# Half of the down projection by seven products instead of eight, in parts of eight middle blocks

## The chip, the cores and the metric

The kernel runs on one core of a Trainium2 chip. Its engines go by the profile's names: PE is TensorE (matmuls; PEld loads their weights), DVE is VectorE, ACT is ScalarE, POOL is GpSimd and SP issues most of the transfers. The metric is device time in microseconds (us), the median of three runs.

## The reference, cut to what matters

Two layers work on 256 tokens of width 2048, all in float32. Each ends with a gated feed-forward block with 5632 middle columns:

```python
h2 = rms_norm(x, ln2_g[l])
u = depthwise_conv(h2 @ w_up[l], conv_w[l], conv_b[l])
gate, up = u[..., :D_FF], u[..., D_FF:]
x = x + (jax.nn.silu(gate) * up) @ w_down[l]
```

Ahead of it stand a norm, one input projection, two groups of attention heads and an output projection. The change touches only the last line, the down projection from 5632 middle columns to 2048 output columns.

## The kernel before

**Two parts of every number.** TensorE works on float32 in a reduced form (float32r). For full precision each operand is split into a high and a low part: `split` has ScalarE copy the source to the high part (L104, tile `whi` for weights) and VectorE subtract it from the source (L105, `wlo`). A product then takes three matmuls: high by high, low by high, high by low. `three` does so for the projections whose weights are the moving operand, with 512 columns each.

**Steps.** All large weights come as 1 MB loads (`quanta`, tile `raw`, three buffers). Each is used in two halves, the steps. `split_w` splits the weights of the step that is four ahead, with priority; `whi` and `wlo` have five buffers, so a split can begin when TensorE has left the step before the present one. The load three ahead is issued when both halves of a load are split.

**Feed-forward block.** The 5632 middle columns are 44 blocks of 128. A block f is made by `q_up` in four steps of 16 matmul pairs, then `glu` turns it into the middle block: ScalarE copies the product from PSUM (L505), VectorE adds and scales (L506, L507), POOL fills the borders of the convolution (L509, L510), ScalarE and VectorE do the convolution (L515, L517), the gate (L519) and the product (L520), and a split makes the two parts, tile `mid`. The down projection works on the four output blocks nb of 512 columns; per nb and pair of middle blocks a step has 12 matmuls (two token halves, two blocks, three products). It runs in chunks of `CHUNKS = (12, 12, 12, 8)` blocks, each chunk behind the up projections of its blocks and of one block more, so that the last block's `glu` is covered. After each nb VectorE adds the PSUM tile to x (`add_x`, L453). PSUM tile `mm` has two buffers of two banks and serves both projections. In the last chunk of a layer nb 0 and nb 1 take turns over the groups of four blocks, as no block follows:

```python
order = [(nb, g) for nb in range(NB) for g in range(ng)]
if end == NF:
    order = sorted(order, key=lambda o: (o[0] // 2, o[1], o[0]) if o[0] < 2 else (1, 0, 0))
```

At the end of the first layer `whole_x` adds to x, squares it and transposes it on TensorE for the next layer (`turn_x`, L140, tile `S`, then `prep_x`, L107 and L108). The order on each engine is set by a scheduler at build time, from the order of the code and the priorities; each engine then works strictly in that order.

Of the kernel before, what the change touches and what calls it, by code (L numbers as in the profile page):

```python
# [11 lines left out]
F32 = mybir.dt.float32  # L12
# [6 lines left out]
P = 128  # L19
# [11 lines left out]
FF = 5632  # L31
NF = FF // P
FG = 4
CHUNKS = (12, 12, 12, 8)
NB = 4
EPS = 1e-6
NEG = -1e30
# [14 lines left out]
def encoder_kernel(  # L52
# [91 lines left out]
    def stat_x(which):  # L144
        v = work.tile([P, TT], F32, name="ssum", bufs=2)
        nc.vector.reduce_sum(v, st["ss"], axis=AX.X)
        st["r1"] = act.tile([P, TT], F32, name="r1")
        rsqrt(v, 1.0 / D, st["r1"], "c2")
        if which == 1:

            d = work.tile([P, 4, HD], F32, name="tq", bufs=2)
            for tt in range(TT):
                nc.vector.tensor_scalar(d[:, tt], ident, st["r1"][:, tt:tt + 1], None, op0=ALU.mult)
            ps = psum.tile([P, T], F32, name="pv", bufs=1)
            mm(ps, ones, d[:, 0:TT].rearrange("p t d -> p (t d)"), True, True)
            st["r2"] = act.tile([P, T], F32, name="r2")
            nc.scalar.activation(st["r2"], ps, AF.Copy)

    def stat_o(grp):
# [197 lines left out]
    def values(l, grp, h):  # L357
        t = sm.pop(("T", grp, h))
        ps = psum.tile([P, T], F32, name="pv", bufs=1)
        if grp == "a":  # L360
            v, c = V["a", h // 4], (h % 4) * HD
            mm(ps[:, 0:KW], v[:, 0, c:c + HD], t[:, 0, 0:KW], True, False)
            mm(ps[:, T - KW:T], v[:, 1, c:c + HD], t[:, 1, 0:KW], False, True)
        else:
            v, c = V["b", 0], (h // 4) * HD
            for kt in range(TT):
                mm(ps, v[:, kt, c:c + HD], t[:, kt, :], kt == 0, kt == TT - 1)
        g = 0 if grp == "a" else 1
        if h == 0:
            acc_o[grp] = act.tile([P, T], F32, name=f"acc_{grp}")  # L370
        k = g * NH + h
        os[k] = act.tile([P, 2, T], F32R, name="mid", bufs=16)
        split(os[k][:, 0], os[k][:, 1], ps, par["on_g"][:, l, g, h:h + 1])
        add_square(acc_o[grp], ps, h == 0)

# [125 lines left out]
    def glu(l, f, ps):  # L501
        ux = halo[f % 2]
        r = T // GRID_W
        t = work.tile([P, 2, T], F32, name="prob", bufs=2)
        nc.scalar.activation(t, ps[:, :, 0], AF.Copy)  # L505
        nc.vector.tensor_add(t, t, ps[:, :, 1])  # L506
        nc.vector.tensor_mul(ux[:, :, r:r + T], t, st["r2"][:, None, :].to_broadcast([P, 2, T]))  # L507

        nc.gpsimd.tensor_copy(ux[:, :, 1:r], ux[:, :, T:T + r - 1])  # L509
        nc.gpsimd.tensor_copy(ux[:, :, T + r:T + 2 * r - 1], ux[:, :, r + 1:2 * r])  # L510
        y = work.tile([P, 2, T], F32, name="pT", bufs=4)
        for j in range(2):
            c = j * NF + f
            w0, w1, w2, b = (par["conv"][:, l, i, c:c + 1] for i in range(4))
            nc.scalar.activation(y[:, j, :], ux[:, j, r:r + T], AF.Identity, scale=w1, bias=b)  # L515
            for w, o in ((w0, 0), (w2, 2 * r)):
                nc.vector.scalar_tensor_tensor(y[:, j, :], ux[:, j, o:o + T], w, y[:, j, :],  # L517
                                               op0=ALU.mult, op1=ALU.add)
        nc.scalar.activation(t[:, 0, :], y[:, 0, :], AF.Silu)  # L519
        nc.vector.tensor_mul(t[:, 1, :], t[:, 0, :], y[:, 1, :])  # L520
        gs[f] = act.tile([P, 2, T], F32R, name="mid", bufs=16)
        split(gs[f][:, 0], gs[f][:, 1], t[:, 1, :])

    def q_down(l, c, nb, g):
        f0, nf = sum(CHUNKS[:c]), CHUNKS[c]

        def body(q, half, hi, lo):
            ps = banks(("dn", nb), g == 0 and half == 0)
            hv, lv = (w.rearrange("p (k n) -> p k n", k=2) for w in (hi, lo))
            i = FG * g + 2 * half  # L530
            three(ps, (gs[f0 + i], gs[f0 + i + 1]), hv, lv, i == 0, i == nf - 2,
# [19 lines left out]
    for l in range(L):  # L551
        for j in range(NJ):
            for u in range(4):
                quanta.append((a["w_in"][l, j, u], q_win(l, j, u), False))
        for grp in "ba":
            for nb in range(NB):
                for u in range(2):
                    quanta.append((a["w_out"][l, 0 if grp == "a" else 1, nb, u], q_wout(l, grp, nb, u), False))
        f = 0
        for c, nf in enumerate(CHUNKS):  # L560

            end = min(sum(CHUNKS[:c + 1]) + 1, NF)
            while f < end:
                for u in range(2):
                    quanta.append((a["w_up"][l, f, u], q_up(l, f, u), True))
                f += 1
            ng = nf // FG
            order = [(nb, g) for nb in range(NB) for g in range(ng)]
            if end == NF:
                order = sorted(order, key=lambda o: (o[0] // 2, o[1], o[0]) if o[0] < 2 else (1, 0, 0))  # L570
            for nb, g in order:
                quanta.append((a["w_down"][l, sum(CHUNKS[:c]) // FG + g, nb], q_down(l, c, nb, g), False))


    steps = [(q, h) for q in range(len(quanta)) for h in range(2)]

    raw, hl, left, loads, highs = {}, {}, {}, {}, {}

    def load(q, parts=1):
        if q < len(quanta):  # L580
            raw[q] = wp.tile([P, 2048], F32, name="raw", bufs=3)
            left[q] = 2
# [20 lines left out]

    xT = []
    for i in range(KD // 2):
        xT.append(act.tile([P, 2, T], F32, name="mid", bufs=16))
# [91 lines left out]
def _layout(inputs):  # L698
# [71 lines left out]
```

## Time and profile before

| | |
|---|---|
| median of three runs | 2126.24 us (2125.97 to 2126.32) |
| profiled execution, time | 2126.1 us |
| its span, first to last instruction | 2124.3 us |
| PE busy | 2118.1 us (100%) |
| DVE busy | 1458.0 us (69%) |
| ACT busy | 1141.2 us (54%) |
| feed-forward stretch of the first layer (345 to 1041 us): PE, DVE, ACT busy | 696.0, 477.6, 363.5 of 696.0 us |
| TensorE clock granted | 1.0 throughout |
| DMA | mean 187 GB/s |

Rows of a timeline give the start, the duration, the engine, the line, what is written from what, and in brackets the idle time before and what ended it. Groups give the busy time, the mean duration in ns and the idle time before. Matmul records overlap: a rate is read from starts. In an unmerged row x8 means eight instructions in a row.

### The profile page before, as it was taken

The page shows a single profiled execution, that of the slowest core. Times are in us where ns is not written, and L with a number is a line of the kernel's source. Part 1 is how long each engine was busy: PE and PEld are TensorE (multiplying, and loading weights), DVE is VectorE, ACT ScalarE, POOL GpSimd, SP SyncE. Part 2 cuts the span into 40 slices and gives each one's busy share as a digit, 9 for nine tenths or more (in the row PEclk, how much of TensorE's full clock was granted, in tenths as well). Part 3 has the DMA queues.
Part 4 walks back from the last instruction along what each step waited for, and adds up shares of the span by engine and source line. Part 5 has one row for each costly group of instructions (what it writes and reads, how often), then busy time and mean ns, then how long its engine had stood idle before and what let it go on. Part 6 is the DMA issues. An engine that isn't in the chain of part 4 may idle for free.

```text
span 2124.3 us, 28802 instructions
## 1 busy us (share of the span) xinstructions
PE 2118.1 (100%) x10904; PEld 1815.3 (85%) x10904; DVE 1458.0 (69%) x2293; ACT 1141.2 (54%) x1651; POOL 142.1 (7%) x215
## 2 busy tenths in 40 slices
PE   9999999999999999999999999999999999999999
PEld 8888888888888888888888888888888888888887
DVE  7777667775677577657756866677756775776575
ACT  7566556554455355535655665565544553555453
POOL 0000000110011011001000000001100100110010
PEclk9999999999999999999999999999999999999999
DMA  9544555555555555555555454555555555555554
GB/s 345 195 141 170 176 178 178 181 197 198 181 196 191 189 195 182 196 198 182 196 180 197 139 171 160 174 182 185 197 194 184 195 188 192 193 185 197 192 185 139
DMA packets 60843, 397.89 MB, mean 187 GB/s; under 512 B 7328, under 2 KB 9888, under 8 KB 13728
## 3 DMA queue, kind: packets, MB, share of 16 engines
q1 hardware_dynamic: 59696, 394.71, 54.3%
q8 instruction: 85, 1.39, 0.3%
q10 hardware_dynamic: 1008, 1.34, 0.2%
q14 instruction: 54, 0.44, 0.1%
HBM read 393.93 MB, written 2.10 MB: 186 GB/s over the span
## 4 chain that ended last, share of the span: by engine, by line
PE 99%; DMA 0%; ACT 0%; DVE 0%; ACTq 0%; DVEq 0%; issue 0%
PE mm L86 95%; PE pv L86 1%; PE S L86 1%; PE tr L292 1%; PE S L140 0%; PE tr L353 0%; PE tr L86 0%; DMA ln_g<-in_ln_g 0%; PE tr L348 0%; PE tr L345 0%; DVE x L546 0%; ACT xs L107 0%; ACT whi L104 0%; ACTq L608 0%; DVEq L765 0%
## 5 line engine op out<-in xcount | busy, mean ns | idle before, releaser
L105 DVE TENSOR_TENSOR wlo<-raw,whi 128x1024 fp32r<-128x1024 f32 (+1 forms) x737 | 901.2, 1223 | 543.8 <-ACT whi L104 504.9
L104 ACT ACTIVATE whi<-raw 128x1024 fp32r<-128x1024 f32 (+1 forms) x737 | 779.7, 1059 | 863.1 <-PE mm L86 671.9
L86 PE MATMUL mm<-xs,whi 128*128 128x512 f32 x2816 | 976.6, 390 | 0.0
L86 PE MATMUL mm<-xs,wlo 128*128 128x256 f32 x2816 | 794.1, 282 | 0.0
L86 PEld LDWEIGHTS mm<-xs,whi 128*128 128x128 f32 x2816 | 528.3, 188 | 110.5
L86 PEld LDWEIGHTS mm<-xs,wlo 128*128 128x128 f32 x2816 | 532.2, 189 | 0.8
L86 PE MATMUL mm<-whi,mid 128*128 128x512 f32 x1920 | 481.5, 391 | 0.0
L86 PEld LDWEIGHTS mm<-whi,mid 128*128 128x128 f32 x1920 | 357.9, 188 | 72.7
L86 PE MATMUL mm<-whi,xs 128*128 128x512 f32 x1152 | 296.3, 395 | 0.7 <-ACT whi L104 0.7
L86 PE MATMUL mm<-wlo,mid 128*128 128x512 f32 x960 | 260.0, 390 | 0.0
L86 PEld LDWEIGHTS mm<-whi,xs 128*128 128x128 f32 x1152 | 214.6, 188 | 45.4 <-ACT whi L104 1.4
L86 PEld LDWEIGHTS mm<-wlo,mid 128*128 128x128 f32 x960 | 180.0, 188 | 37.2
L86 PE MATMUL mm<-wlo,xs 128*128 128x512 f32 x576 | 162.0, 396 | 0.0
L517 DVE SCALAR_TENSOR_TENSOR pT<-halo,conv,pT 128x256 f32<-128x256 f32 x352 | 146.7, 479 | 0.5
L86 PEld LDWEIGHTS mm<-wlo,xs 128*128 128x128 f32 x576 | 107.3, 188 | 21.7 <-DVE wlo L105 0.4
L509 POOL COPY halo<-halo 128x6 f32<-128x6 f32 x88 | 22.7, 258 | 1359.8 <-DVE halo L507 1359.8
L515 ACT ACTIVATE pT<-halo,conv 128x256 f32<-128x256 f32 x176 | 95.1, 588 | 0.2
L510 POOL COPY halo<-halo 128x6 f32<-128x6 f32 x88 | 95.1, 1081 | 0.2 <-POOL halo L509 0.2
L507 DVE TENSOR_TENSOR halo<-prob,r 128x512 f32<-128x512 f32 x88 | 60.9, 692 | 2.7
L506 DVE TENSOR_TENSOR prob<-prob,mm 128x512 f32<-128x512 f32 x88 | 59.9, 681 | 0.0
L453 DVE TENSOR_TENSOR x<-x,mm 128x1024 f32<-128x1024 f32 x28 | 34.2, 1221 | 35.3 <-PE mm L86 35.3
L505 ACT ACTIVATE prob<-mm 128x512 f32<-128x512 f32 x88 | 51.1, 581 | 0.0
(129 smaller groups left out, 857.8 us busy)
## 6 DMA issues: line engine op xcount, KB each, us to landing
raw<-in_w_up SPq DMA_DIRECT2D x176, 1024.0 KB, 4.8
raw<-in_w_down SPq DMA_DIRECT2D x88, 1024.0 KB, 4.8
raw<-in_w_in SPq DMA_DIRECT2D x71, 1024.0 KB, 4.9
raw<-in_w_out SPq DMA_DIRECT2D x32, 1024.0 KB, 4.8
bias<-in_bias SPq DMA_DIRECT2D x16, 160.0 KB, 3.8
x<-in_x SPq DMA_DIRECT2D x4, 512.0 KB, 8.9
out<-x SPq DMA_DIRECT2D x6, 256.0 KB, 2.5
mid<-in_xT ACTq DMA_DIRECT2D x4, 256.0 KB, 6.2
```

The lines of the kernel that those rows point to most:

```text
L86: nc.tensor.matmul(ps, lhsT, rhs, start=start, stop=stop, skip_group_check=True)
L104: high = nc.scalar.activation(hi, src, AF.Copy)
L105: nc.vector.tensor_sub(lo, src, hi.bitcast(F32))
L292: nc.tensor.transpose(ps[:, j, tt * P:(tt + 1) * P], qn[tt][:, p + j, :], ident)
L453: nc.vector.tensor_add(xv, xv, ps)
L505: nc.scalar.activation(t, ps[:, :, 0], AF.Copy)
L506: nc.vector.tensor_add(t, t, ps[:, :, 1])
L507: nc.vector.tensor_mul(ux[:, :, r:r + T], t, st["r2"][:, None, :].to_broadcast([P, 2, T]))
L509: nc.gpsimd.tensor_copy(ux[:, :, 1:r], ux[:, :, T:T + r - 1])
L510: nc.gpsimd.tensor_copy(ux[:, :, T + r:T + 2 * r - 1], ux[:, :, r + 1:2 * r])
L515: nc.scalar.activation(y[:, j, :], ux[:, j, r:r + T], AF.Identity, scale=w1, bias=b)
L517: nc.vector.scalar_tensor_tensor(y[:, j, :], ux[:, j, o:o + T], w, y[:, j, :], op0=ALU.mult, op1=ALU.add)
```

## The change

The down projection now goes in five parts of eight blocks and one of four. In a part of eight, output blocks 2 and 3 are computed as before. Output blocks 0 and 1 are computed from pairs of middle blocks: the two blocks of a pair, the two token halves and the two output blocks make a 2x2 by 2x2 product, done with seven products of sums (Winograd's form of Strassen's scheme) instead of eight. One of the seven enters only one corner; its weights, for four pairs, are gathered in `w_plain` (two steps of 6 matmuls). The other six are `q_seven`: one load per pair holds the four weight blocks, used in three steps of 6 matmuls, and collects the products over the four pairs in six PSUM banks, an `mm` tile and the banks of `S`, `tr` and `pv`. `add_seven` adds them to x.

The sums cost work on VectorE: `sums_mid` makes four sums of half blocks for each pair and splits them into two more `mid` tiles; `split_seven` makes three sums of weights in the `raw` tile, in place, ahead of the second step's split. The order of a part is plain, then four times a seven and one load of blocks 2 and 3, which now share one PSUM tile with plain. The last part has four blocks and goes over nb in order. `mid` has 17 buffers for 16, and `r2` takes the room of `acc_b`.

```diff
--- before.py
+++ after.py
@@ -31,7 +31,11 @@
-CHUNKS = (12, 12, 12, 8)
+
+
+PART = 8
+CHUNKS = (8, 8, 8, 8, 8, 4)
+MIDS = 17
...
@@ -517,15 +521,96 @@
                 nc.vector.scalar_tensor_tensor(y[:, j, :], ux[:, j, o:o + T], w, y[:, j, :],
                                                op0=ALU.mult, op1=ALU.add)
         nc.scalar.activation(t[:, 0, :], y[:, 0, :], AF.Silu)
-        nc.vector.tensor_mul(t[:, 1, :], t[:, 0, :], y[:, 1, :])
-        gs[f] = act.tile([P, 2, T], F32R, name="mid", bufs=16)
-        split(gs[f][:, 0], gs[f][:, 1], t[:, 1, :])
+        m = work.tile([P, T], F32, name="bias", bufs=2)
+        nc.vector.tensor_mul(m, t[:, 0, :], y[:, 1, :])
+        gs[f] = act.tile([P, 2, T], F32R, name="mid", bufs=MIDS)
+        split(gs[f][:, 0], gs[f][:, 1], m)
+        ms[f] = m
+        if f % 2 and f < NF // PART * PART:
+            sums_mid(f // 2, ms.pop(f - 1), ms.pop(f))
+
+    ms, ss = {}, {}
+
+    def sums_mid(p, m1, m2):
+
+        a, b = slice(0, P), slice(P, T)
+        v = work.tile([P, 4, HD], F32, name="tq", bufs=2)
+        nc.vector.tensor_add(v[:, 0], m1[:, b], m2[:, b])
+        nc.vector.tensor_sub(v[:, 1], v[:, 0], m1[:, a])
+        nc.vector.tensor_sub(v[:, 2], m1[:, a], m1[:, b])
+        nc.vector.tensor_sub(v[:, 3], m2[:, a], v[:, 1])
+        for i in range(2):
+            t = act.tile([P, 2, T], F32R, name="mid", bufs=MIDS)
+            split(t[:, 0], t[:, 1], v[:, 2 * i:2 * i + 2].rearrange("p j n -> p (j n)"))
+            for j in range(2):
+                ss[p, 2 * i + j] = t[:, :, j * P:(j + 1) * P]
+
+    def q_seven(l, c, i):
+
+        f = sum(CHUNKS[:c]) + 2 * i
+        p = f // 2
+        a, b = slice(0, P), slice(P, T)
+
+        def body(q, part, hi, lo):
+            if i == 0 and part == 0:
+                t = psum.tile([P, 2, 512], F32, name="mm", bufs=2)
+                ps = {1: t[:, 0], 6: t[:, 1]}
+                for n, name, k in ((5, "S", 2), (7, "S", 2), (3, "tr", 1), (4, "pv", 1)):
+                    ps[n] = psum.tile([P, 512], F32, name=name, bufs=k)
+                cur["seven"] = ps
+            ps = cur["seven"]
+            hv, lv = (w.rearrange("p (k n) -> p k n", k=2) for w in (hi, lo))
+            todo = (((3, ss[p, 3]), (1, gs[f][:, :, a])),
+                    ((7, ss[p, 2]), (5, ss[p, 0])),
+                    ((4, gs[f + 1][:, :, b]), (6, ss[p, 1])))[part]
+            for j, (n, x2) in enumerate(todo):
+                for x_part, w in ((0, hv), (1, hv), (0, lv)):
+                    mm(ps[n], x2[:, x_part], w[:, j], i == 0 and x_part == 0 and w is hv,
+                       i == PART // 2 - 1 and w is lv)
+            if i == PART // 2 - 1 and part == 2:
+                with tc.high_priority(offset=AHEAD_PRIO):
+                    add_seven(ps)
+        return body
+
+    def add_seven(ps):
+
+        t = work.tile([P, 512], F32, name="sqx", bufs=1)
+        x11, x12 = x[:, 0, 0:512], x[:, 0, 512:1024]
+        x21, x_2, x2_ = x[:, 1, 0:512], x[:, :, 512:1024], x[:, 1, 0:1024].rearrange("p (j n) -> p j n", j=2)
+        both = lambda v: v[:, None, :].to_broadcast([P, 2, 512])
+        nc.vector.tensor_add(x11, x11, ps[1])
+        nc.scalar.activation(t, ps[1], AF.Copy)
+        nc.vector.tensor_add(t, t, ps[6])
+        nc.vector.tensor_add(x12, x12, t)
+        nc.vector.tensor_add(x12, x12, ps[3])
+        nc.vector.tensor_add(x_2, x_2, both(ps[5]))
+        nc.vector.tensor_add(t, t, ps[7])
+        nc.vector.tensor_add(x2_, x2_, both(t))
+        nc.vector.tensor_sub(x21, x21, ps[4])
+
+    def q_plain(l, c):
+
+        f0 = sum(CHUNKS[:c])
+
+        def body(q, half, hi, lo):
+            if half == 0:
+                cur["dn"] = psum.tile([P, TT, 512], F32, name="mm", bufs=2)
+            ps = cur["dn"][:, 0]
+            hv, lv = (w.rearrange("p (k n) -> p k n", k=2) for w in (hi, lo))
+            for x_part, w in ((0, hv), (1, hv), (0, lv)):
+                for i in range(2):
+                    mm(ps, gs[f0 + 4 * half + 2 * i + 1][:, x_part, 0:P], w[:, i],
+                       half == 0 and i == 0 and x_part == 0 and w is hv, half == 1 and i == 1 and w is lv)
+            if half == 1:
+                xv = x[:, 0, 0:512]
+                nc.vector.tensor_add(xv, xv, ps)
+        return body
 
     def q_down(l, c, nb, g):
         f0, nf = sum(CHUNKS[:c]), CHUNKS[c]
 
         def body(q, half, hi, lo):
-            ps = banks(("dn", nb), g == 0 and half == 0)
+            ps = cur["dn"] if nf == PART else banks(("dn", nb), g == 0 and half == 0)
             hv, lv = (w.rearrange("p (k n) -> p k n", k=2) for w in (hi, lo))
             i = FG * g + 2 * half
             three(ps, (gs[f0 + i], gs[f0 + i + 1]), hv, lv, i == 0, i == nf - 2,
...
@@ -551,50 +636,67 @@
...
         f = 0
         for c, nf in enumerate(CHUNKS):
 
             end = min(sum(CHUNKS[:c + 1]) + 1, NF)
             while f < end:
                 for u in range(2):
-                    quanta.append((a["w_up"][l, f, u], q_up(l, f, u), True))
+                    quanta.append((a["w_up"][l, f, u], q_up(l, f, u), "up"))
                 f += 1
-            ng = nf // FG
-            order = [(nb, g) for nb in range(NB) for g in range(ng)]
-            if end == NF:
-                order = sorted(order, key=lambda o: (o[0] // 2, o[1], o[0]) if o[0] < 2 else (1, 0, 0))
-            for nb, g in order:
-                quanta.append((a["w_down"][l, sum(CHUNKS[:c]) // FG + g, nb], q_down(l, c, nb, g), False))
-
-
-    steps = [(q, h) for q in range(len(quanta)) for h in range(2)]
+            down = lambda nb, g: (a["w_down"][l, sum(CHUNKS[:c]) // FG + g, nb], q_down(l, c, nb, g), "")
+            if nf == PART:
+                quanta.append((a["w_plain"][l, c], q_plain(l, c), ""))
+                for i in range(PART // 2):
+                    quanta.append((a["w_seven"][l, c, i], q_seven(l, c, i), "seven"))
+                    quanta.append(down(2 + i // 2, i % 2))
+            else:
+                for nb in range(NB):
+                    for g in range(nf // FG):
+                        quanta.append(down(nb, g))
+
+
+    steps = [(q, h) for q in range(len(quanta)) for h in range(3 if quanta[q][2] == "seven" else 2)]
 
...
-            left[q] = 2
+            left[q] = 3 if quanta[q][2] == "seven" else 2
...
+    def split_seven(w, part, hi, lo):
+
+        hv, lv = (t.rearrange("p (k n) -> p k n", k=2) for t in (hi, lo))
+        if part == 1:
+            nc.vector.tensor_sub(w[:, 1:3], w[:, 1:3], w[:, 2:4])
+            nc.vector.tensor_add(w[:, 3], w[:, 3], w[:, 1])
+            nc.vector.tensor_sub(w[:, 0], w[:, 3], w[:, 0])
+        return split(hv, lv, (w[:, 1::2], w[:, 1:3], w[:, 0::3])[part])
+
     def split_w(s, parts=1):
         if s < len(steps):
             q, half = steps[s]
-            at_ = UP_AT if quanta[q][2] else 0
-            hl[s] = tuple(wp.tile([P, 1024 + 64], F32R, name=t, bufs=SPLIT_AHEAD + 1)[:, at_:at_ + 1024]
+            kind = quanta[q][2]
+            o = UP_AT if kind == "up" else 0
+            hl[s] = tuple(wp.tile([P, 1024 + 64], F32R, name=t, bufs=SPLIT_AHEAD + 1)[:, o:o + 1024]
                           for t in ("whi", "wlo"))
-            m = 1024 // parts
-            for j in range(parts):
-                with tc.high_priority(offset=AHEAD_PRIO if s >= KD // 2 else 0):
-                    highs[s] = split(*(t[:, j * m:(j + 1) * m] for t in hl[s]),
-                                     raw[q][:, half * 1024 + j * m:half * 1024 + (j + 1) * m])
+            with tc.high_priority(offset=AHEAD_PRIO if s >= KD // 2 else 0):
+                if kind == "seven":
+                    highs[s] = split_seven(raw[q].rearrange("p (k n) -> p k n", k=4), half, *hl[s])
+                else:
+                    m = 1024 // parts
+                    for j in range(parts):
+                        highs[s] = split(*(t[:, j * m:(j + 1) * m] for t in hl[s]),
+                                         raw[q][:, half * 1024 + j * m:half * 1024 + (j + 1) * m])
             left[q] -= 1
             if left[q] == 0:
                 del raw[q]
...
@@ -726,6 +828,13 @@
         L, 2, NB, 2, P, 2048)
     o["w_up"] = c(f["w_up"].reshape(L, 2, 8, P, 2, NF, P).transpose(0, 5, 1, 3, 2, 4, 6)).reshape(
         L, NF, 2, P, 2048)
+    wd = f["w_down"]
+    n = NF // PART
+
+    four = wd[:, :n * PART * P, :1024].reshape(L, n, PART // 2, 2, P, 2, 512)
+    o["w_seven"] = c(np.stack([four[:, :, :, k, :, m] for k, m in ((1, 0), (1, 1), (0, 1), (0, 0))], 4)).reshape(
+        L, n, PART // 2, P, 2048)
+    o["w_plain"] = c(four[:, :, :, 1, :, 0].transpose(0, 1, 3, 2, 4)).reshape(L, n, P, 2048)
     o["w_down"] = c(f["w_down"].reshape(L, NF // FG, FG, P, NB, 512).transpose(0, 1, 4, 3, 2, 5)).reshape(
         L, NF // FG, NB, P, 2048)
```

What the scheduler makes of it is seen on VectorE in the down projection of a part. Before (a chunk of the first layer; wlo is a split, L453 the addition of an output block to x):

```order
L105 TENSOR_TENSOR mid<-prob,mid 128x256
L105 TENSOR_TENSOR wlo<-raw,whi 128x1024
L453 TENSOR_TENSOR x<-x,mm 128x2x512
L105 TENSOR_TENSOR wlo<-raw,whi 128x1024 x6
L453 TENSOR_TENSOR x<-x,mm 128x2x512
```

Now, at the start of the second seven of a part (L109 is `split`, L680 to L682 the sums of weights, L521 the convolution, L525 the gated product, L540 a sum of middle blocks):

```order
L109 TENSOR_TENSOR wlo<-raw,whi 128x1024
L521 SCALAR_TENSOR_TENSOR pT<-halo_110,conv,pT 128x256 x2
L680 TENSOR_TENSOR raw<-raw 128x1024
L525 TENSOR_TENSOR bias<-prob,pT 128x256
L681 TENSOR_TENSOR raw<-raw 128x512
L540 TENSOR_TENSOR tq<-bias 128x128
L682 TENSOR_TENSOR raw<-raw 128x512
L109 TENSOR_TENSOR wlo<-raw,whi 128x1024
```

The three sums of weights stand between the first and the second split of the seven, with pieces of the next middle block's work between them.

And at the end of the part, on VectorE (L581 to L589 are the additions of `add_seven`, L457 that of output block 3):

```order
L109 TENSOR_TENSOR wlo<-raw,whi 128x1024 x5
L581 TENSOR_TENSOR x<-x,mm 128x512
L109 TENSOR_TENSOR wlo<-raw,whi 128x1024
L583 TENSOR_TENSOR sqx<-sqx,mm 128x512
L109 TENSOR_TENSOR wlo<-raw,whi 128x1024
L584 TENSOR_TENSOR x<-x,sqx 128x512
L457 TENSOR_TENSOR x<-x,mm 128x2x512
L109 TENSOR_TENSOR wlo<-raw,whi 128x1024
L585 TENSOR_TENSOR x<-x,tr 128x512
L587 TENSOR_TENSOR sqx<-sqx,S 128x512
```

The additions stand one by one between splits for the next up projection, where an addition to x stood alone before.

The third place is TensorE at the end of the first layer. Before (mid_8887 is the last middle block, made by the last up projection, 67 matmuls earlier; mm_8894 and mm_8929 are output blocks 0 and 1):

```order
L86 MATMUL mm_8894<-whi_8907,mid_8784 128x512
L86 MATMUL mm_8929<-whi_8925,mid_8578 128x512
L86 MATMUL mm_8929<-whi_8925,mid_8681 128x512
L86 MATMUL mm_8929<-whi_8925,mid_8578 128x512
L86 MATMUL mm_8929<-whi_8925,mid_8681 128x512
L86 MATMUL mm_8929<-whi_8925,mid_8578 128x512
L86 MATMUL mm_8929<-whi_8925,mid_8681 128x512
L86 MATMUL mm_8894<-whi_8907,mid_8887 128x512
```

Now (mid_9488 is the last middle block, mm_9495 and mm_9531 are output blocks 0 and 1):

```order
L90 MATMUL mm_9531<-wlo_9431,mid_8860 128x512
L90 MATMUL mm_9531<-wlo_9431,mid_9280 128x512
L90 MATMUL mm_9531<-whi_9450,mid_9384 128x512
L90 MATMUL mm_9495<-whi_9408,mid_9488 128x512
L90 MATMUL mm_9495<-whi_9408,mid_9384 128x512
L90 MATMUL mm_9495<-whi_9408,mid_9488 128x512
```

Between the last up projection and the first matmul that reads the last middle block there now stand 26 matmuls: 12 and 12 on the first pair for output blocks 0 and 1, and one of each on the third block.

More of the change, by code (lines that the diff above doesn't have):

```diff
@@ L155, in stat_x @@
             mm(ps, ones, d[:, 0:TT].rearrange("p t d -> p (t d)"), True, True)
-            st["r2"] = act.tile([P, T], F32, name="r2")
+            st["r2"] = act.tile([P, T], F32, name="acc_b")
             nc.scalar.activation(st["r2"], ps, AF.Copy)
@@ L371, in values @@
         k = g * NH + h
-        os[k] = act.tile([P, 2, T], F32R, name="mid", bufs=16)
+        os[k] = act.tile([P, 2, T], F32R, name="mid", bufs=MIDS)
         split(os[k][:, 0], os[k][:, 1], ps, par["on_g"][:, l, g, h:h + 1])
@@ L553, in encoder_kernel @@
             for u in range(4):
-                quanta.append((a["w_in"][l, j, u], q_win(l, j, u), False))
+                quanta.append((a["w_in"][l, j, u], q_win(l, j, u), ""))
         for grp in "ba":
@@ L557, in encoder_kernel @@
                 for u in range(2):
-                    quanta.append((a["w_out"][l, 0 if grp == "a" else 1, nb, u], q_wout(l, grp, nb, u), False))
+                    quanta.append((a["w_out"][l, 0 if grp == "a" else 1, nb, u], q_wout(l, grp, nb, u), ""))
         f = 0
@@ L605, in encoder_kernel @@
     for i in range(KD // 2):
-        xT.append(act.tile([P, 2, T], F32, name="mid", bufs=16))
+        xT.append(act.tile([P, 2, T], F32, name="mid", bufs=MIDS))
         if i < 4:
```

## The prediction

> **What bounds the kernel now.** I read the page first: busy times, the chain that ended last, the costliest groups.
>
> ```profile
> span 2124.3 us, 28802 instructions
> PE 2118.1 (100%) x10904; PEld 1815.3 (85%) x10904; DVE 1458.0 (69%) x2293; ACT 1141.2 (54%) x1651; POOL 142.1 (7%) x215
> PE 99%; DMA 0%; ACT 0%; DVE 0%; ACTq 0%; DVEq 0%; issue 0%
> L105 DVE TENSOR_TENSOR wlo<-raw,whi 128x1024 fp32r<-128x1024 f32 (+1 forms) x737 | 901.2, 1223 | 543.8 <-ACT whi L104 504.9
> L104 ACT ACTIVATE whi<-raw 128x1024 fp32r<-128x1024 f32 (+1 forms) x737 | 779.7, 1059 | 863.1 <-PE mm L86 671.9
> raw<-in_w_down SPq DMA_DIRECT2D x88, 1024.0 KB, 4.8
> ```
>
> TensorE is 99% of the chain. VectorE's splits mostly wait for ScalarE's (504.9 us), and those for TensorE to free a buffer (671.9 us): both run as far ahead as the buffers allow. Fewer matmuls therefore shorten the run one for one, as long as VectorE (69%, the next) keeps its lead in the part that gets the new work. So I went on to the timeline of a down projection.
>
> ```profile
> 503.49 1.98 PE L86 MATMUL mm<-whi,mid 128*128 128x512 f32 x8
> 505.31 1.07 PE L86 MATMUL mm<-wlo,mid 128*128 128x512 f32 x4
> 506.21 1.98 PE L86 MATMUL mm<-whi,mid 128*128 128x512 f32 x8
> 511.85 1.22 DVE L453 TENSOR_TENSOR x<-x,mm 128x1024 f32<-128x1024 f32 x1 [1.31 <-PE mm L86]
> 512.99 1.22 DVE L105 TENSOR_TENSOR wlo<-raw,whi 128x1024 fp32r<-128x1024 f32 x1
> ```
>
> A step of 12 matmuls takes 506.21 - 503.49 = 2.72 us, so a matmul of 512 columns costs 0.2267 us; the 0.39 us of its own record overlaps the next. The last two rows show the same on VectorE: an operation already queued starts 1.14 us after the one before, though that is recorded with 1.22.
>
> Then one block of the up projection, VectorE alone:
>
> ```profile
> 567.71 1.23 DVE L105 TENSOR_TENSOR wlo<-raw,whi 128x1024 fp32r<-128x1024 f32 x1 [1.20 <-ACT whi L104]
> 568.85 0.68 DVE L506 TENSOR_TENSOR prob<-prob,mm 128x512 f32<-128x512 f32 x1
> 569.57 0.69 DVE L507 TENSOR_TENSOR halo<-prob,r 128x512 f32<-128x512 f32 x1
> 570.50 1.23 DVE L105 TENSOR_TENSOR wlo<-raw,whi 128x1024 fp32r<-128x1024 f32 x1 [0.24 <-ACT whi L104]
> 571.64 1.67 DVE L517 SCALAR_TENSOR_TENSOR pT<-halo,conv,pT 128x256 f32<-128x256 f32 x4
> 573.26 1.23 DVE L105 TENSOR_TENSOR wlo<-raw,whi 128x1024 fp32r<-128x1024 f32 x1
> 574.40 0.42 DVE L520 TENSOR_TENSOR prob<-prob,pT 128x256 f32<-128x256 f32 x1
> 576.04 1.23 DVE L105 TENSOR_TENSOR wlo<-raw,whi 128x1024 fp32r<-128x1024 f32 x1 [1.22 <-ACT whi L104]
> 577.19 0.42 DVE L105 TENSOR_TENSOR mid<-prob,mid 128x256 fp32r<-128x256 f32 x1
> 578.81 1.22 DVE L105 TENSOR_TENSOR wlo<-raw,whi 128x1024 fp32r<-128x1024 f32 x1 [1.20 <-ACT whi L104]
> ```
>
> A block takes 578.81 - 567.71 = 11.1 us; VectorE is idle 0.24 + 1.22 + 1.20 = 2.7 us of it and needs 8.4. An operation that reads what the one before wrote starts 0.72 us after it (568.85 to 569.57), 0.04 more than its duration. The shortest kind comes from the groups kept apart by shape:
>
> ```profile
> L196 DVE SCALAR_TENSOR_TENSOR tq<-tq 128x128 f32<-128x128 f32 x26 | 7.4, 290 | 0.6
> ```
>
> So I have two prices per VectorE operation: queued and independent (duration less 0.085: 1.14 for 1024 elements, 0.60 for 512, 0.33 for 256, 0.20 for 128) and dependent (duration plus 0.04: 1.27, 0.72, 0.46, 0.33).
>
> **The change, part by part.** *Matmuls.* Two output blocks over a pair of middle blocks took 24 matmuls; now six products take 18, and the seventh, gathered in w_plain, 3 per pair. That saves 3 x 4 pairs x 5 parts x 2 layers = 120 matmuls: 120 x 0.2267 = **-27.2 us**. No unknown is in this.
>
> *The end of a layer.* Before, 8 blocks end the layer, and two output blocks are interleaved so that the last middle block is first wanted 67 matmuls (15.2 us) after its up projection. Now the last part has 4 blocks, and it is wanted after 26 (5.9 us). What that block needs is in the timeline of the first layer's end:
>
> ```profile
> 1018.68 0.28 PE L86 MATMUL mm<-xs,wlo 128*128 128x256 f32 x1
> 1019.89 0.58 ACT L505 ACTIVATE prob<-mm 128x512 f32<-128x512 f32 x1
> 1021.16 0.68 DVE L506 TENSOR_TENSOR prob<-prob,mm 128x512 f32<-128x512 f32 x1
> 1021.97 1.23 DVE L105 TENSOR_TENSOR wlo<-raw,whi 128x1024 fp32r<-128x1024 f32 x1
> 1023.11 0.69 DVE L507 TENSOR_TENSOR halo<-prob,r 128x512 f32<-128x512 f32 x1
> 1024.05 0.19 POOL L510 COPY halo<-halo 128x6 f32<-128x6 f32 x1
> 1024.55 1.08 ACT L515 ACTIVATE pT<-halo,conv 128x256 f32<-128x256 f32 x2
> 1025.82 1.67 DVE L517 SCALAR_TENSOR_TENSOR pT<-halo,conv,pT 128x256 f32<-128x256 f32 x4
> 1027.29 0.40 ACT L519 ACTIVATE prob<-pT 128x256 f32<-128x256 f32 x1
> 1027.72 0.42 DVE L520 TENSOR_TENSOR prob<-prob,pT 128x256 f32<-128x256 f32 x1 [0.23 <-ACT prob L519]
> 1029.27 0.40 ACT L104 ACTIVATE mid<-prob 128x256 fp32r<-128x256 f32 x1
> ```
>
> From the last matmul's end (1018.96) to the high half (1029.67) it took 10.7 us, with splits of weights between. At that pace TensorE waits 10.7 - 5.9 = 4.8 us; if only the chain's own durations counted (0.58 + 0.68 + 0.69 + 0.3 + 1.08 + 1.67 + 0.40 + 0.42 + 0.40 = 6.2) it waits 0.3. In the new order ScalarE has two weight splits fewer inside the chain and VectorE one more behind the convolution; walking the rows with that, L507's operation ends at 4.8 (as before), the convolution at 7.3, a split at 8.4, the product at 8.8, the high half at 9.3: 3.4 us, and as much in the second layer. In the first layer the transposes of the finished x stand in TensorE's queue right behind the first two output blocks, and the addition they wait for stands on VectorE behind a split whose buffer comes free late: 11 matmuls after the wait (11.8), copy, split and addition (1.06 + 1.14 + 1.22, and hops) end at 15.4, TensorE is there at 14.3: 1.1 more (0 to 2.5). Together **+8 us**. Everything behind the waiting matmul on TensorE is queued with it, and no other engine wants that sooner.
>
> *VectorE's work per part of eight.* Down part: 22 splits instead of 16 (25.1 us at 1.14), raw sums 4 x (1.14 + 0.60 + 0.60) = 9.4, additions to x (plain 0.6, two of 1.14, the eight of add_seven 5.9) 8.8: 43.3 us, against TensorE's 12 + 72 + 96 = 180 matmuls, 40.8 us. The sums of the middle blocks add some 1.7 us per pair (two splits at 0.33, four sums of 128) to 22.2 us of up projection, where 5.4 are idle: hidden. ScalarE gets 6 more splits and small copies at 54%: hidden; if VectorE's cover goes, it waits with it. The ten added loads have 40.8 / 9 = 4.5 us each in the down part, against 4.8 to land and three buffers: hidden, at most a wait of the same size as VectorE's.
>
> So the down part alone wants 2.5 us more of VectorE than of TensorE, and pays from the lead. Whether that suffices is decided where the demand comes earliest. I set zero where TensorE starts the part. By the order, VectorE's queue from the end of the last convolution group to the last raw sum of the second seven holds 6 splits, 6 raw sums, 3 operations of 512, 5 of 256, 4 of the convolution and 4 of 128: 6.8 + 4.7 + 1.8 + 1.7 + 1.6 + 0.8 = 17.4 us at queued prices, 20.5 at dependent ones. The group ends 6.7 us after its block's last matmul (573.31 against 566.65, with the 2.2 us from the last matmul to L506 of the rows above, 1021.16 - 1018.96), which lies 11.1 before zero: it ends at -4.4. So that sum ends at 13.0, and the high half that ScalarE then makes (1.06 us) is there at 14.1. TensorE reaches its use after 12 + 18 + 24 + 6 + 4 = 64 matmuls, at 14.5. At dependent prices it is there at 17.2 and TensorE waits 2.7. Bounds per part: 0 and 2.7 us. The scheduler has put other work between most dependent pairs, so I take a value near the lower end, 0.6: ten parts, **+6 us**. The later sevens have more room by the same count (x of block 2 is added about 1.3 us before its bank is reused). At the part's end the next up block takes the bank that is free once add_seven has added product 6, not that of the last addition to x, so nothing is paid there.
>
> The Trainium skill ("VectorE: DVE Perf Modes", The DRAIN you can't avoid) says that a next operation does not start until the pipe is empty, and that one should keep the count of operations small; by it the dependent price would hold for all, and the part would lose 2.7 us. The 1.14 us above speaks against it for operations that are not held, as that page's own later section allows.
>
> Sum: -27.2 + 6 + 8 = -13.2 us. The profiled execution took 2126.1 us for its span of 2124.3; its median over three runs is 2126.24, so the same sum holds for both: **2113 us**. At the bounds: -27.2 + 0.6 = -26.6 (2099.6) and -27.2 + 27 + 12.1 = +11.9 (2138).
>
> **The rivals.** *VectorE becomes the bound in the down part* (slower). Place: the raw sums of the second seven; price: the dependent prices, 2.7 us a part, with the later sevens and the bank of the next up block then late too, some 0.5 more (4 x 0.085 and six additions): 3.2 x 10 = 32; 2124.3 - 27.2 + 8 + 32 = 2137, about 2139 us. It decides from 1.9 us a part on, where the gain is gone. For it: 43.3 against 40.8 us, sums written in place one behind the other. Against it: the overlap in the trace and the order's interleaving.
> *The two costs eat the gain* (no change): 1.5 to 2.3 us a part, or 4.8 at each layer end and 1.4 a part: 2122 to 2130.
> *The layer ends are covered after all*: as forecast without the 8 us, 2105 us. Against it: the 26 matmuls stand in the order, and the chain's own durations already exceed them.
>
> **How the numbers follow.** Forecast 0.57 (its own range 2107 to 2121: a stall of 0 to 1.3 us a part), covered layer ends 0.06, gain eaten 0.15, VectorE the bound 0.22. A measurement of this kernel can tell some 0.2% (4.3 us) from no change. Faster: 0.57 + 0.06 and a sliver of the third case, 0.64; same 0.13; slower 0.23. The range 2104 to 2137 leaves out the tops of the slower case and the very best.
>
> **What would show it.** Right: PE x10784 on the page, 120 fewer; TensorE idle 3 to 5 us once at the end of each layer, waiting for the middle block's high half; TensorE waiting under 1.3 us a part, for a high half of a second seven; VectorE near 80%. Wrong: waits for wlo or whi in every seven, or a long wait at the first up block behind a part (the bank), or a down part longer than 42.5 us; no idle time at the layer ends; or matmuls of the sevens spaced other than 0.2267 us.

## The result, and the profile after

The changed kernel takes 2111.26 us (2111.1 to 2113.7, 4 runs), the kernel before 2126.28 us beside it (2125.97 to 2126.45, 4 runs): ratio 0.9932, 95% interval 0.9916 to 0.9948, faster by 15.0 us. The profiled execution took 2111.1 us, with a span of 2109.3 us.

The page of the changed kernel, the rows that answer to those shown of before (L90 is now the matmul, L108 and L109 are the two halves of a split):

```profile
span 2109.3 us, 29266 instructions
PE 2095.8 (99%) x10784; PEld 1794.3 (85%) x10784; DVE 1737.5 (82%) x2799; ACT 1224.0 (58%) x1801; POOL 134.8 (6%) x215
PE 99%; DVE 0%; ACT 0%; DMA 0%; issue 0%; ACTq 0%; DVEq 0%
L109 DVE TENSOR_TENSOR wlo<-raw,whi 128x1024 fp32r<-128x1024 f32 (+1 forms) x797 | 964.2, 1220 | 272.4 <-ACT whi L108 234.2
raw<-in_w_seven SPq DMA_DIRECT2D x40, 1024.0 KB, 4.9
```

TensorE has 120 matmuls fewer, and is still 99% of the chain. VectorE went from 69% to 82%, and the idle time before its splits from 543.8 to 272.4 us: half of this spare time is gone. What TensorE waited for is in the view of waits (total, times, longest), first of the changed kernel, then of the kernel before:

```profile
PE mm L90 <- ACT mid L108: 6.1, 2, 3.1
PE pv L90 <- DVE halfpi L86: 1.1, 1, 1.1
PE S L144 <- DVE x L457: 1.0, 1, 1.0
PE mm L90 <- ACT whi L108: 0.8, 1, 0.8
...
PE pv L86 <- DVE halfpi L82: 1.1, 1, 1.1
PE mm L86 <- ACT whi L104: 0.7, 1, 0.7
```

The two rows that both kernels have end at 1.1 and 7.7 us, at the very start. New are the two waits for a middle block's high half, one at each layer end, and the one at the transposes. No row speaks of a seven: the down parts wait for nothing. The first part's down projection by window (PE, PEld, DVE, ACT and POOL busy, then clock and DMA):

```profile
434.75:475.59 40.84, 40.84 (x182) 33.76 (x181) 40.14 (x48) 25.27 (x30) 1.18 (x2) 1.00 0.58 208
```

TensorE is busy for all of the 40.84 us (180 matmuls at 0.2267 us are 40.81), VectorE for 40.14. The place where the prediction saw the lead run out, the second seven, on VectorE, ScalarE and TensorE of the changed kernel:

```profile
447.20 0.68 DVE L682 TENSOR_TENSOR raw<-raw 128x512 f32<-128x512 f32 x1
447.80 1.21 DVE L109 TENSOR_TENSOR wlo<-raw,whi 128x1024 fp32r<-128x1024 f32 x1
...
447.99 3.90 ACT L108 ACTIVATE whi<-raw 128x1024 fp32r<-128x1024 f32 x4 [0.39 <-DVE raw L682]
...
449.27 0.63 PE L90 MATMUL pv<-whi,mid 128*128 128x512 f32 x2
```

The last raw sum gives way to the next operation at 447.80, 13.05 us after the part's start at 434.75 (worked out: 13.0). The first of the four high halves is there some 1.06 us after 447.99, at 449.05, 14.3 us into the part (worked out: 14.1), and used at 449.27 (14.5). The lead is 0.2 us here, in the first part.

The end of the first layer, TensorE, with the windows of one microsecond behind the wait (the next to last three numbers are the granted clock, the DMA share and GB/s):

```profile
1029.90 2.51 PE L90 MATMUL mm<-whi,mid 128*128 128x512 f32 x9
1032.24 1.08 PE L90 MATMUL mm<-wlo,mid 128*128 128x512 f32 x4
1033.16 0.39 PE L90 MATMUL mm<-whi,mid 128*128 128x512 f32 x1
1036.59 4.38 PE L90 MATMUL mm<-whi,mid 128*128 128x512 f32 x11 [3.03 <-ACT mid L108]
1040.80 1.08 PE L90 MATMUL mm<-wlo,mid 128*128 128x512 f32 x4
1041.72 0.85 PE L90 MATMUL mm<-whi,mid 128*128 128x512 f32 x3
1042.41 1.07 PE L90 MATMUL mm<-wlo,mid 128*128 128x512 f32 x4
1044.51 1.09 PE L144 MATMUL S<-ident,x 128*128 128x128 f32 x8 [1.03 <-DVE x L457]
```

```profile
1036.00:1037.00 1.00, 0.41 (x2) 0.37 (x3) 0.51 (x2) 0.42 (x1) 0.00 (x0) 1.00 0.35 127
1037.00:1038.00 1.00, 1.00 (x5) 0.76 (x4) 0.00 (x0) 0.00 (x0) 0.00 (x0) 0.58 0.01 1
1038.00:1039.00 1.00, 1.00 (x4) 0.81 (x3) 0.00 (x0) 0.00 (x0) 0.00 (x0) 0.50 0.59 163
1039.00:1040.00 1.00, 1.00 (x4) 0.80 (x3) 0.00 (x0) 0.00 (x0) 0.00 (x0) 0.50 0.00 0
1040.00:1041.00 1.00, 1.00 (x4) 0.75 (x4) 0.00 (x0) 0.00 (x1) 0.00 (x0) 0.71 0.00 0
1041.00:1042.00 1.00, 1.00 (x6) 0.80 (x5) 0.00 (x0) 1.00 (x1) 0.00 (x0) 1.00 0.00 0
```

The wait of 3.03 us and the 1.03 us at the transposes are those that were foreseen. What follows the wait was not: the granted clock falls to 0.50, and 11 matmuls take 1040.80 - 1036.59 = 4.21 us instead of 11 x 0.2267 = 2.49. That is 1.7 us lost, and the windows give the same (0.42 + 0.50 + 0.50 + 0.29 = 1.71). At the end of the second layer 16 matmuls behind a wait of 3.08 us take 5.36 us instead of 3.63: 1.7 us again.

So the account of the 15.0 us became, as a theory to be tried: matmuls -27.2, VectorE's work next to nothing, two waits +6.1, transposes +1.0, half clock behind the waits +3.4, and about 1 us of small gaps around them (the 9 matmuls from 1029.90 take 2.34 us instead of 2.04; from the last start before the wait to the first behind it there are 3.43 us, 0.17 more than the wait and one matmul). These terms add up to -15.7 us; the other 0.7 us is in none of them.

### The profile page after: what moved, and what is told of

Its sections match the earlier page's. It is cut to its first block, busy times and chain, and to the rows that moved or that the text cites. A ratio compares the mean times of both kernels' runs of the same rounds, so it can differ in the third digit from the quotient of the medians.

```text
span 2109.3 us, 29266 instructions
## 1 busy us (share of the span) xinstructions
PE 2095.8 (99%) x10784; PEld 1794.3 (85%) x10784; DVE 1737.5 (82%) x2799; ACT 1224.0 (58%) x1801; POOL 134.8 (6%) x215
## 4 chain that ended last, share of the span: by engine, by line
PE 99%; DVE 0%; ACT 0%; DMA 0%; issue 0%; ACTq 0%; DVEq 0%
PE mm L90 89%; PE S L90 4%; PE pv L90 2%; PE tr L90 2%; PE tr L296 1%; PE S L144 1%; PE tr L357 0%; DMA ln_g<-in_ln_g 0%; DVE wlo L109 0%; ACT whi L108 0%; DVE pT L521 0%; PE tr L352 0%; PE tr L349 0%; DVE halo L511 0%; ACT pT L519 0%
## 5 line engine op out<-in xcount | busy, mean ns | idle before, releaser
L108 ACT ACTIVATE whi<-raw 128x1024 fp32r<-128x1024 f32 (+1 forms) x797 | 829.7, 1056 | 681.1 <-PE mm L90 423.3
L109 DVE TENSOR_TENSOR wlo<-raw,whi 128x1024 fp32r<-128x1024 f32 (+1 forms) x797 | 964.2, 1220 | 272.4 <-ACT whi L108 234.2
L90 PE MATMUL mm<-xs,whi 128*128 128x512 f32 x2816 | 976.8, 390 | 0.0
L90 PE MATMUL mm<-xs,wlo 128*128 128x256 f32 x2816 | 794.1, 282 | 0.0
L90 PEld LDWEIGHTS mm<-xs,whi 128*128 128x128 f32 x2816 | 528.3, 188 | 110.5
L90 PEld LDWEIGHTS mm<-xs,wlo 128*128 128x128 f32 x2816 | 532.2, 189 | 0.9
L90 PE MATMUL mm<-whi,mid 128*128 128x512 f32 x1520 | 399.1, 394 | 6.1 <-ACT mid L108 6.1
L90 PEld LDWEIGHTS mm<-whi,mid 128*128 128x128 f32 x1520 | 284.2, 189 | 65.4 <-ACT mid L108 7.0
L90 PE MATMUL mm<-whi,xs 128*128 128x512 f32 x1152 | 297.2, 395 | 0.8 <-ACT whi L108 0.8
L90 PEld LDWEIGHTS mm<-whi,xs 128*128 128x128 f32 x1152 | 214.3, 188 | 45.4 <-ACT whi L108 1.6
L90 PE MATMUL mm<-wlo,mid 128*128 128x512 f32 x760 | 215.7, 392 | 0.0
L90 PEld LDWEIGHTS mm<-wlo,mid 128*128 128x128 f32 x760 | 142.9, 188 | 29.7
L90 PE MATMUL mm<-wlo,xs 128*128 128x512 f32 x576 | 162.2, 396 | 0.0
L521 DVE SCALAR_TENSOR_TENSOR pT<-halo,conv,pT 128x256 f32<-128x256 f32 x352 | 147.5, 478 | 2.6 <-ACT pT L519 1.5
L513 POOL COPY halo<-halo 128x6 f32<-128x6 f32 x88 | 38.3, 435 | 1383.9 <-DVE halo L511 1383.9
L90 PEld LDWEIGHTS mm<-wlo,xs 128*128 128x128 f32 x576 | 107.3, 188 | 21.7 <-DVE wlo L109 0.4
L514 POOL COPY halo<-halo 128x6 f32<-128x6 f32 x88 | 72.0, 819 | 0.0
L511 DVE TENSOR_TENSOR halo<-prob,acc_b 128x512 f32<-128x512 f32 x88 | 60.6, 689 | 1.9
L523 ACT ACTIVATE prob<-pT 128x256 f32<-128x256 f32 x88 | 35.7, 405 | 35.0 <-DVE pT L521 34.9
```

The lines of the kernel that those rows point to most:

```text
L90: nc.tensor.matmul(ps, lhsT, rhs, start=start, stop=stop, skip_group_check=True)
L108: high = nc.scalar.activation(hi, src, AF.Copy)
L109: nc.vector.tensor_sub(lo, src, hi.bitcast(F32))
```

## The experiments

In the edited kernels a line has another number where lines were added above it: L91 in the kernel with unread matmuls is L90 here, and L695 is the third raw sum.

**Layer ends covered.** If the three costs of the layer ends are real, another order of the same work takes them all away. The last three up projections go in between the third and the fourth seven of the last part of eight, and that part's last output block behind them:

```diff
+            late = c == len(CHUNKS) - 2 and nb == NB - 1
-            ps = cur["dn"] if nf == PART else banks(("dn", nb), ...)
+            ps = cur["dn"] if nf == PART and not late else banks(("dn", nb), ...)
...
+                if c < len(CHUNKS) - 2:
...
+                else:
+                    quanta += [plain, seven[0], down(2, 0), seven[1], down(2, 1), seven[2],
+                               up(f, 0), seven[3], up(f, 1), up(f + 1, 0), up(f + 1, 1), up(f + 2, 0), up(f + 2, 1),
+                               down(3, 0), down(3, 1)]
+                    f = NF
```

> The changed kernel with the end of each layer in another order: the last three up projections stand between the third and the fourth seven's loads of the last part of eight, and that part's last output block (48 matmuls, 10.9 us) behind them, so the last middle block is wanted after 74 matmuls (16.8 us) and not after 26 (5.9 us). Theory (layer ends cost the wait of 3.0 us, about 1 us at the transposes of the first layer and 1.7 to 2 us of matmuls at a lower granted clock behind each wait): all three go, 6.1 + 1.0 + 3.7 = 10.8 us less than the changed kernel, about 2100.5 us. Rival (the lower clock is not from the wait but from elsewhere): only 7.1 go, about 2104. Rival (the end of the layer is bound by VectorE and the wait comes back at another place): 2108 to 2112.

Measured: 2099.72 us (2099.53 to 2100.73), ratio to before 0.9876 (0.9862 to 0.9889). Its waits:

```profile
PE mm L90 <- ACT whi L108: 1.3, 1, 1.3
PE pv L90 <- DVE halfpi L86: 1.1, 1, 1.1
```

The rows for the middle block and the transposes are gone, and the time falls by 11.5 us, not by the 7.1 of the waits alone. This version beats both kernels. It also measures the sevens by themselves, since neither it nor the kernel before has an open layer end: spans 2097.7 against 2124.3, -26.6 us, of the -27.2 worked out (0.2 us of the difference is there after 28 us, ahead of any seven).

**Only the clock.** Thirteen matmuls that nobody reads stand in front of the wait and keep TensorE busy through it; the wait ends no sooner.

```diff
+FILL = 13
...
+            if nf < PART and nb == 0 and half == 1:
+                idle = psum.tile([P, 512], F32, name="tr", bufs=1)
+                for _ in range(FILL):
+                    mm(idle, gs[f0][:, 0, 0:P], hv[:, 0], True, True)
```

> The changed kernel with 13 matmuls that nobody reads (2.95 us at 0.2267 us each, into the free bank tr) in front of the matmul that waits for the last middle block, at each layer end. The wait for that block's high half ends when it did, but TensorE is idle for 0.1 us of it and not for 3.0. Theory (the matmuls behind the wait run slowly because TensorE stood idle): the 11 matmuls behind it take 2.5 us again and not 4.2, the windows behind it show a granted clock of 1.0 and not 0.57 to 0.65, and the time falls by 3 to 4 us to about 2107.5. Rival (they are slow for another reason, such as what the other engines do at that time): clock, 4.2 us and 2111 us stay.

Measured: 2107.1 us (2106.91 to 2107.23). Same place, the matmuls and the windows behind the wait:

```profile
1036.50 2.81 PE L91 MATMUL mm<-whi,mid 128*128 128x512 f32 x11 [0.37 <-ACT mid L109]
1039.15 1.07 PE L91 MATMUL mm<-wlo,mid 128*128 128x512 f32 x4
```

```profile
1037.00:1038.00 1.00, 1.00 (x6) 0.78 (x5) 0.74 (x2) 0.00 (x0) 0.00 (x0) 1.00 0.00 0
1038.00:1039.00 1.00, 1.00 (x6) 0.82 (x5) 0.00 (x0) 0.00 (x0) 0.00 (x0) 1.00 0.21 29
```

The high half comes at the same time (1036.50 for 1036.59), and the 11 matmuls behind it take 2.65 us, at full clock. So without the idle time there is no half clock, with the same matmuls before and after it. The 4.2 us gained are not all clock: the wait at the transposes is gone as well, because VectorE's queue now has the addition ahead of a split and not behind it, an effect of the edit that was not foreseen.

**Eight products in the same parts.** The kernel before with the new division into parts alone:

```diff
-CHUNKS = (12, 12, 12, 8)
+CHUNKS = (8, 8, 8, 8, 8, 4)
```

> The kernel before with parts of 8, 8, 8, 8, 8 and 4 and nothing else: eight products for eight, the layer ends as the changed kernel has them. It differs from the changed kernel by the sevens alone. Theory (the sevens save 120 matmuls, 27.2 us, and cost nothing; the layer ends cost all of the rest): the changed kernel's time + 27.2, about 2138.5 us, with idle time of 3 us at both layer ends. Rival (the layer ends cost their two waits and the transposes alone, 7 us, and the sevens lose some 5 us of their own): about 2133.5.

Measured: 2136.82 us (2135.14 to 2138.36), slower than before by 10.5 us (ratio 1.005, 1.0038 to 1.0063). Its waits show the two layer ends and nothing else that is new:

```profile
PE mm L86 <- ACT mid L104: 6.1, 2, 3.1
```

So the smaller parts cost this by themselves, with no seven in the kernel. The time lies between the two expectations, nearer to the theory; the runs of this kernel spread over 3.2 us, so this pair does not tell 25.6 from 27.2 for the sevens. The covered kernel does (above).

**How much lead VectorE has.** Two sums that nobody reads, ahead of the raw sums of the first seven of a part:

```diff
+        if part == 1 and first:
+            t = work.tile([P, 512], F32, name="sqx", bufs=1)
+            nc.vector.tensor_sub(t, w[:, 1], w[:, 2])
+            nc.vector.tensor_sub(t, w[:, 2], w[:, 3])
```

> The changed kernel with two more sums of 512 elements on VectorE (0.60 us each, read by nobody) ahead of the raw sums of the first seven of each of the ten parts: 1.2 us a part. In the changed kernel's trace the high half of the second seven's third step is there at 449.05 and used at 449.27, a margin of 0.22 us, and VectorE runs without idle time from 428 to 472. Theory (the lead is used up to 0.2 us): TensorE now waits about 1.2 - 0.2 = 1.0 us a part, 10 us in all, about 2121 us. Rival (VectorE has a reserve of over 1.2 us, since queued work closes up or other work moves): no wait, 2111 us.

Measured: 2111.83 us (2109.68 to 2113.48), no change, as the rival said. But the trace shows that this dose of added work missed the place: nothing tied the sums to it, and the scheduler set them into the up projection ahead, where VectorE was idle for 1.20 us in the changed kernel.

```profile
422.07 1.23 DVE L109 TENSOR_TENSOR wlo<-raw,whi 128x1024 fp32r<-128x1024 f32 x1 [0.90 <-ACT whi L108]
423.21 0.68 DVE L683 TENSOR_TENSOR sqx<-raw 128x512 f32<-128x512 f32 x1
...
424.15 0.68 DVE L684 TENSOR_TENSOR sqx<-raw 128x512 f32<-128x512 f32 x1
424.83 1.23 DVE L109 TENSOR_TENSOR wlo<-raw,whi 128x1024 fp32r<-128x1024 f32 x1
```

It shows only that work which can move ahead is free. So the next dose was put into the chain itself, on top of the covered kernel, whose times spread less: a maximum of a tensor with itself, between the raw sums.

```diff
             nc.vector.tensor_sub(w[:, 1:3], w[:, 1:3], w[:, 2:4])
+            if second:
+                nc.vector.tensor_max(w[:, 1:3], w[:, 1:3], w[:, 1:3])
```

> The kernel with the covered layer ends (2099.7 us) and one more operation on VectorE in the chain of raw sums of the second seven of each of the ten parts: a maximum of 1024 elements with itself, which changes no value. It adds 1.14 us there, and the new order puts a low half of 1024 and one of 256 (1.14 and 0.33 us) ahead of the third sum too: the high half of the third step comes 2.6 us later. Theory (the lead at this place is 0.2 us, 449.05 against 449.27 in the changed kernel): TensorE waits 2.4 us in each part for that high half, 24 us in all, about 2124 us. Rival (VectorE has a reserve there that the trace does not show): under 0.5 us a part, 2100 to 2105 us.

Measured: 2120.47 us (2120.32 to 2120.69), 20.8 us more than the covered kernel, 2.1 a part for the 2.4 expected. ScalarE and TensorE at the second seven:

```profile
450.74 2.96 ACT L108 ACTIVATE whi<-raw 128x1024 fp32r<-128x1024 f32 x3 [1.98 <-DVE raw L695]
...
448.82 1.19 PE L90 MATMUL S<-whi,mid 128*128 128x512 f32 x4 [0.29 <-ACT whi L108]
450.08 0.73 PE L90 MATMUL S<-wlo,mid 128*128 128x512 f32 x2
451.85 0.73 PE L90 MATMUL pv<-whi,mid 128*128 128x512 f32 x2 [1.04 <-ACT whi L108]
```

The high half starts at 450.74, against 448.08 in the covered kernel: 2.66 us later, as worked out. TensorE's order put the two matmuls of S with the low half (0.45 us) in front, which covers a part. The recorded idle time is 1.33 us here and 1.22 a part on average; the rest shows as matmuls that start further apart around the waits (four of S take 1.26 us, not 0.91). Taken together, 2.66 - 0.45 - 0.2 = 2.0 us, against 2.1 measured: there was no hidden reserve, and the lead at this place is the 0.2 us of the trace.

The same maximum in all four sevens of a part (the condition left out):

> As the kernel before this one, with the added maximum in all four sevens of a part, 4 x 1.14 to 1.27 us. Theory (VectorE paces the down part from here on; margins of 0.2 us at the second seven and 1.0 to 1.2 us at the third and fourth): 4.8 - 1.0 = 3.8 us a part, 38 us in all, about 2138 us, slower than the kernel before; no wait stays behind in the up projections, where VectorE is idle for 2.7 us a block. Rival (a reserve of over 1 us a seven): 2100 to 2110 us.

Measured: 2141.77 us (2141.03 to 2142.49), ratio to before 1.0073 (1.0058 to 1.0088), 42 us more than the covered kernel, 4.2 a part. The recorded waits hold 24.4 of it:

```profile
PE S L90 <- ACT whi L108: 13.4, 15, 1.4
PE pv L90 <- ACT whi L108: 11.0, 22, 1.7
```

This is the prediction's slower rival, brought about by one operation more a seven. Then the other side: a kernel that leaves out the three raw sums, and so multiplies by the unsummed weights.

> The kernel with the covered layer ends without the three raw sums of the weights of each seven (9.4 us of VectorE a part, 94 us in all; the products then use the wrong weights). Theory (VectorE's work costs TensorE nothing as it stands): the same time, 2099 to 2100 us. The prediction's choice (0.6 us of waiting a part): about 2094 us.

Measured: 2099.17 us (2099.13 to 2099.44), 0.55 us less than the covered kernel, for 84 us less work on VectorE (busy 1652.8 us, not 1736.9). So the raw sums cost TensorE at most half a microsecond in all as the kernel stands; less can't be told, since the covered kernel's runs lie 1.2 us apart, and of the 0.4 us between the two profiled spans 0.18 is there after 28 us, ahead of any raw sum.

**How long TensorE may idle.** Six unread matmuls for thirteen (FILL = 6):

> The changed kernel with 6 unread matmuls (1.36 us) in place of the 13 in front of the wait at each layer end: TensorE is idle for about 1.7 us there, where 3.0 us lowered the clock and 0.37 us did not. Reading one (the clock falls only when the idle time passes a length that lies above 1.7 us): the matmuls behind run at full pace, the same time as with 13, about 2107 us. Reading two (what is lost grows with the idle time): half the loss, about 2109 us. Reading three (1.7 us is as bad as 3.0): about 2111 us.

Measured: 2107.63 us; but the four runs are 2106.63, 2106.79, 2108.48 and 2108.6. The profiled one is of the faster pair:

```profile
1036.63 2.79 PE L91 MATMUL mm<-whi,mid 128*128 128x512 f32 x11 [2.11 <-ACT mid L109]
1039.26 1.07 PE L91 MATMUL mm<-wlo,mid 128*128 128x512 f32 x4
```

TensorE is idle for 2.1 us, more than the 1.7 worked out, and the clock stays at 1.00 (11 matmuls in 2.63 us). The other two runs are 1.8 us longer, about what one stretch at half clock costs; the mean clock on record for them is 0.999, against 1.0 for the shorter two, which fits, but runs of the kernel before show both values with no difference in time. As the two have no trace, this cause is argued, not shown. No reading holds in every run.

## Why the prediction was right, and where it was not

2113 us was predicted and 2111.26 measured. The matmuls and the waits at the layer ends came as they were named; the wait in the down part, which the forecast also held, did not come, and something that it did not hold made up for most of that. By its terms:

- *Matmuls, -27.2.* Right: 10784 of them, 40.84 us a down part, -26.6 us in all between two kernels with covered layer ends, and -27.0 without the raw sums (2124.3 to 2097.3).
- *VectorE in the down part, +6.* Mis-sized: the changed kernel's trace shows no wait there, and with the layer ends covered the raw sums cost at most 0.55. The working itself was right to 0.2 us: 13.0 and 14.1 worked out, 13.05 and 14.3 measured, 14.5 needed. The step that failed is the last one, "a value near the lower end, 0.6": the count said no wait, and the 0.6 was set against the dependent price. Of the two prices, the queued one held at this place: the split behind the third sum starts 0.60 us after it, though that is recorded with 0.68. Where sums do stand one behind the other, in the third and fourth seven, the dependent price holds, and there the trace shows no wait either:

```profile
453.93 1.23 DVE L680 TENSOR_TENSOR raw<-raw 128x1024 f32<-128x1024 f32 x1
455.19 0.69 DVE L681 TENSOR_TENSOR raw<-raw 128x512 f32<-128x512 f32 x1
455.91 0.69 DVE L682 TENSOR_TENSOR raw<-raw 128x512 f32<-128x512 f32 x1
```

  These are 1.26 and 0.72 us apart, as the prices say. The doses show that the caution was not idle: a high half that came 2.66 us later at one place cost 2.1 us a part, and one operation more a seven made the change a loss. (The forecast's own range, a stall of 0 to 1.3 us a part, ends at 2120 by its terms, not at 2121.)
- *Layer ends, +8.* The waits were right: 3.03 and 3.08 us (3.4 worked out), transposes 1.03 (1.1), 7.1 us together. The chain from the last matmul to the high half took 9.2 us (9.3).
- *Missing: the half clock behind the two waits, +3.4, and some 1 us around them.* The prediction read the granted clock nowhere. The trace of before shows no TensorE wait that long while work is left. But its clock is not 1.0 to the very end: the last matmul ends at 2119.87, and in the windows of one microsecond from 2123 to 2126 the granted clock is 0.50. That row could have warned of the effect.

So the two errors, 6 us too much and about 4.4 too little, nearly cancel. That the total came within 2 us is to this extent luck. The rival with covered layer ends named a price of 8 us for them; the true one was 11.5.

## What to carry to other kernels

When an engine is at 98% in a stage, count its queue up to the operation whose deadline comes first, at the prices of queued work, and believe the count: here it was right to 0.2 us, and extra work was free ahead of that place and mostly paid within it (2.1 of 2.6 us). A stall of TensorE at the start of a last, short part can cost more than its length (here 11.5 us for 7.1 us of waits); look for other ready work to put between the last producer and its first reader, which here was worth 11.5 us beside the change's 15.0. To test a lead, tie the added work into the chain, or the scheduler will move it to where it costs nothing.

## What the runs showed of the hardware

A wait of 3.0 us was enough to halve TensorE's granted clock, and the half rate came in whole stretches: 1.7 us lost, or 3.4 us at 0.50, at each layer end of the changed kernel. In the kernel with the two unread sums both stretches were twice as long, 6.8 us (1036.0 to 1042.8 and 2087.3 to 2094.1 by the windows). The first, by its windows:

```profile
1036.00:1038.00 2.00, 1.13 (x3) 0.95 (x4) 0.79 (x3) 0.42 (x1) 0.00 (x0) 0.50 0.24 89
1038.00:1040.00 2.00, 2.00 (x6) 1.56 (x5) 0.00 (x0) 0.00 (x0) 0.00 (x0) 0.50 0.29 82
1040.00:1042.00 2.00, 2.00 (x6) 1.61 (x5) 0.00 (x0) 0.03 (x1) 0.00 (x0) 0.50 0.00 0
1042.00:1044.00 2.00, 2.00 (x8) 1.60 (x8) 0.57 (x1) 1.02 (x1) 0.00 (x0) 0.79 0.00 0
```

The times of the five runs of this kernel are 2109.68, 2111.67, 2111.83, 2111.87 and 2113.48 us, steps of about one stretch, while the covered kernel's four lie within 1.2 us; the profiled one is the longest, the others have no trace. The Trainium skill ("TensorE: Matmul & The Clock Gate", Part 1: The HAM clock gate) has it that activity is judged in free-running windows of some 3.4 us, half rate following an idle window and full rate a busy one. The length of the stretches agrees (3.4 us), and where they begin fits a window that runs freely: 0.6 us behind the wait's end in the changed kernel (1037.16 against 1036.59) and 0.9 us ahead of it in this one (1036.0 against 1036.87). But 3.0 us of idle time sufficed here at both layer ends of the trace. In the kernel with the maximum in every seven, waits of 1.08 and 0.57 us that lie close together went with a clock of 0.73:

```profile
449.50 1.19 PE L90 MATMUL S<-whi,mid 128*128 128x512 f32 x4 [1.08 <-ACT whi L108]
451.26 0.73 PE L90 MATMUL pv<-whi,mid 128*128 128x512 f32 x2 [0.57 <-ACT whi L108]
```

```profile
450.00:454.00 4.00, 3.43 (x11) 2.40 (x11) 4.00 (x6) 3.85 (x4) 0.00 (x0) 0.73 0.25 33
```

while in the one with six unread matmuls 2.11 us in one piece left the clock at 1.00 in the profiled run. In the 3.4 us ahead of each fall TensorE was idle for 2.8 and 2.0 us at the two layer ends of the changed kernel, 2.2 at the first of the kernel with two unread sums, and 1.6 in the kernel with the maximum in every seven. So, if the clock is judged over such a stretch, it needs not be wholly idle, and the 2.11 us may have lain across two of them; no run here places the windows, and how much idle time lowers the clock stays open.
